# The second modulation's weights loaded ahead of the gathers and in the second front, with front weights in four slots and the first expert weights requested behind its attention

## The chip, the cores and the metric

The kernel runs on one core of a Trainium2 chip. The metric is the time of one execution on the device in microseconds (us). A measurement of it is the median of some runs of the same program. Weights, tables and inputs start in HBM, the output ends there. The core has five engines with a queue of instructions each: PE (matmuls), DVE and ACT (elementwise work, reductions, casts), POOL (it issues the indirect gathers here) and SP (it issues the plain loads). Sixteen DMA engines move all the data. An engine takes its queue in order, so an instruction that waits holds up all that stand behind it.

## The reference, cut to what matters

256 tokens of width 1024 go through two blocks.

```python
# first block (after attention and a recurrent branch)
mod = silu(c) @ w_ada + b_ada                        # 6 x 1024
h2 = rms_norm(x) * (1 + scale2) + shift2
q = (h2 @ w_query).reshape(128, 8, 2, 128)           # 8 heads, two halves
s_top, i_top = top_k(q . sub_keys, 16)               # of 128 keys each
best, pos = top_k(sums of the two, 16)               # of 256 pairs
idx, g = i_top[0] * 128 + i_top[1], softmax(best)    # 16 of 16384 experts
x += gate2 * sum_k g * gelu(x . expert_u[idx]) * expert_v[idx]

# second block
mod_2 = silu(c_2) @ w_ada_2 + b_ada_2                # sh1, sc1, ga1, sh2, sc2, ga2
h = rms_norm(x) * (1 + sc1) + sh1
q, k, v, xb, bg, cg, gates = split(h @ w_in_2)       # 5120 columns
y_a, y_b = attention(rope(q), rope(k), v), gated_conv(xb, bg, cg)
x += ga1 * ((gate_a * (y_a @ w_pa) + gate_b * (y_b @ w_pb)) @ w_o)
x += ga2 * moe(rms_norm(x) * (1 + sc2) + sh2)        # 32 experts, w1, w3, w2
```

The vector c_2 is an input: mod_2 depends on nothing that the first block computes.

## The kernel before

The kernel runs in stages: the first front (`_front1`), the scores of the first expert layer (`_peer_scores`), its experts (`_peer_experts`), the second front (`_front2`) and the second expert layer (`_moe`). All large weights go through one SBUF buffer, `arena`, of eight slots of 128 x 4096 float32 (2 MB, called a piece here); two more slots, 8 and 9, exist only from the second expert layer on. The first is the buffer `room` of the second front under another use.

**Loads.** SP issues every piece in the order of its queue; a load waits until all who used the slot are done, and all loads behind it in the queue wait with it. For the second block `load2` takes slots from a fixed sequence (`ring`, L169): first 3, 4, 5, 6, 0, 7 in turn, then ten slots in turn. It issues a piece when it is first asked for. A scheduler sets the order of the instructions on each engine from the dependences and its own estimates; the order written in the program is where it starts from.

**Gathers.** `_peer_experts` treats each block of 128 tokens in 32 groups of four gathers. A gather (L838) fetches 128 rows of 8 KB, 1.05 MB, each row the two vectors u and v of an expert. Ten buffers take turns: seven quarter-slot pairs in the arena (in slots 0, 1, 5, 6 and 7) and three tiles named `uv`. For each gather PE spreads a token's row over a wide PSUM tile `bc` (L855; there are two of these), DVE multiplies it with u and sums (L857), and for each group PE adds the weighted v into `acc` (L864). The buffer is then free.

**Routing.** The list of picks per block (`route`) is DVE work handed out in small slices by `k.fill`. Block 0's is done in full before the first gather: `k.fill(1e9, (0,))`. It ends with a transpose on PE of the picks (L789), whose copy is the gathers' index table `idx`; a second one (L796) makes the weights `gT`. Block 1's is done beside block 0's groups, a slice of 4.5 us by its own estimate behind each (`k.fill(4.5, (1,))`). Its tables fill slot 4 and part of slot 5. PE's transposes at L811 (`by_tokens`) turn the tokens for the broadcasts.

**Second modulation.** w_ada_2 has twelve pieces. Three calls of `modulation2`, behind groups 4, 12 and 20 of block 0 in program order, take four pieces each through slots 3 and 2 in turn. A piece is eight matmuls (16 rows of the trace, which shows each of these float32 products as two) with c_2's column vectors (`csr2`, L206) into a PSUM bank; behind the fourth, ACT copies the bank (`ada_m`), PE transposes it (L217) and DVE adds the bias into `mod2`. On SP, pieces 0 and 1 are issued at the end of the scores, and the scheduler has put all twelve into the first fifteen groups.

**Second front.** The statistics of x come first (L233, eight matmuls), then the modulated x, then q, k and v (L286 to L288, three matmuls for each product, 144 in all), the rotation of q and k on DVE (L295 to L312), heads (L363), attention, then 14 projections of 48 matmuls each (L273 to L275; the scheduler puts them among the attention), the products with w_pa and w_pb, the router and w_o. The ten pieces of w_in_2 are used in order of their number. The order on PE is the scheduler's.

## Time and profile before

| | |
|---|---|
| time, median of 3 runs | 1730.04 us (1729.21 to 1736.62) |
| the profiled execution, its own time | 1729.57 us |
| its span | 1727.8 us |
| busy: PE, DVE, ACT, POOL | 1319.6, 854.9, 309.2, 241.4 us |
| moved by DMA | 594.56 MB, mean 344 GB/s |
| of these plain loads (queue q1), gathers (q0) | 324.80 MB, 268.45 MB |

The span runs from the first to the last instruction that the profiler saw; the 1.8 us beside it are the start and the end of the execution. A stretch in which the DMA share is 1.00 is one in which all sixteen engines always had a packet to move. The granted clock is that of TensorE, as a share of its full 2.4 GHz.

### The profile page before, as it was taken

The numbers are of one execution on the slowest core, as the hardware profiler recorded it, in microseconds if no ns is written. First come the engines' busy times: TensorE is split into PE (matmuls) and PEld (weight loads), VectorE is DVE, ScalarE is ACT, GpSimd is POOL, SyncE is SP. The second block draws the span as 40 slices with busy tenths as digits, with TensorE's granted clock in tenths as the row PEclk, the third lists the DMA queues.
The fourth block names the chain that finished last, engine by engine and source line by source line (L and its number), as shares of the span: only waits on it lengthen the run. The fifth ranks groups of instructions, "written<-read, shape, count | busy, mean of one in ns | idle before, by whom it ended". The sixth has DMA issues, their size and how long they took to land.

```text
span 1727.8 us, 19564 instructions
## 1 busy us (share of the span) xinstructions
PE 1319.6 (76%) x7782; PEld 775.2 (45%) x7782; DVE 854.9 (49%) x1844; ACT 309.2 (18%) x545; POOL 241.4 (14%) x260
## 2 busy tenths in 40 slices
PE   4999999466777777778767775999989666665765
PEld 2878899322332333333333332799964212221211
DVE  4778778938872454454545454775443211120111
ACT  3566544110000000010000001545230000000000
POOL 0000000033332234333433330000000000000000
PEclk8999999778888889898998887999989978888888
DMA  9467741189999999999999998445479999999997
GB/s 379 191 244 274 307 175 50 49 363 419 420 423 424 420 420 421 420 420 420 420 420 419 420 416 329 154 147 201 145 301 427 428 426 428 427 428 427 427 427 306
DMA packets 64992, 594.56 MB, mean 344 GB/s; under 512 B 7008, under 2 KB 8064, under 8 KB 12672
## 3 DMA queue, kind: packets, MB, share of 16 engines
q1 hardware_dynamic: 28032, 324.80, 46.0%
q0 software_dynamic: 36864, 268.45, 37.5%
q8 instruction: 63, 1.03, 0.2%
q14 instruction: 33, 0.27, 0.0%
HBM read 592.15 MB, written 1.08 MB: 343 GB/s over the span
## 4 chain that ended last, share of the span: by engine, by line
DMA 48%; PE 31%; DVE 13%; issue 3%; ACT 2%; POOL 1%; SPq 0%; DVEq 0%; POOLq 0%; ACTq 0%
DMA arena<-w 18%; DMA arena<-uv,idx 16%; DMA uv<-uv,idx 8%; DMA ring<-w 5%; PE acc L864 4%; PE ps L275 3%; PE ps L273 3%; PE bc L855 3%; PE ps L274 3%; DVE arena L857 3%; DVE wl L262 2%; PE ps L980 2%; DVE uv L857 2%; PE ps L1195 1%; POOL arena L838 1%
## 5 line engine op out<-in xcount | busy, mean ns | idle before, releaser
L855 PE MATMUL bc<-ht,identr 128*128 128x512 f32 x1024 | 336.6, 456 | 173.0 <-DVE arena L857 115.6
L855 PEld LDWEIGHTS bc<-ht,identr 128*128 128x128 f32 x1024 | 189.4, 206 | 358.5 <-DVE arena L857 173.5
L857 DVE SCALAR_TENSOR_TENSOR arena<-arena,bc 128x1024 f32<-128x1024 f32 x181 | 219.7, 1219 | 216.1 <-DMA arena<-uv,idx 136.5
L838 POOL DMA_INDIRECT arena<-uv,idx x181 | 170.3, 941 | 706.1 <-DVE arena L793 348.3
L273 PE MATMUL ps<-hr,wh 128*128 128x256 f32 x648 | 183.3, 283 | 0.9 <-ACT wh L261 0.8
L275 PE MATMUL ps<-hr,wl 128*128 128x256 f32 x648 | 182.0, 281 | 0.4 <-DVE wl L262 0.4
L274 PE MATMUL ps<-hr,wh 128*128 128x256 f32 x648 | 181.9, 281 | 0.0
L262 DVE TENSOR_TENSOR wl<-arena,wh 128x1024 fp32r<-128x1024 f32 (+1 forms) x116 | 139.5, 1213 | 74.4 <-ACT wh L261 73.9
L864 PE MATMUL acc<-arena,wz 128*32 128x512 f32 x724 | 162.4, 776 | 6.0 <-DVE wz L860 6.0
L1195 PE MATMUL ps<-arena,xg 128*32 128x512 f32 x832 | 116.0, 687 | 55.3 <-DMA arena<-w 55.1
L261 ACT CAST wh<-arena 128x1024 fp32r<-128x1024 f32 (+1 forms) x116 | 119.6, 1043 | 137.4 <-PE ps L274 95.4
L857 DVE SCALAR_TENSOR_TENSOR uv<-uv,bc 128x1024 f32<-128x1024 f32 x75 | 91.3, 1219 | 88.6 <-PE bc L855 45.0
L273 PEld LDWEIGHTS ps<-hr,wh 128*128 128x128 f32 x648 | 121.9, 188 | 5.1 <-ACT wh L261 2.3
L275 PEld LDWEIGHTS ps<-hr,wl 128*128 128x128 f32 x648 | 121.8, 188 | 1.6 <-DVE wl L262 0.8
L274 PEld LDWEIGHTS ps<-hr,wh 128*128 128x128 f32 x648 | 121.9, 188 | 0.7 <-issue 0.5
L858 ACT ACTIVATE s<-s 128x4 f32<-128x4 f32 x64 | 13.1, 205 | 606.4 <-DVE arena L857 346.9
L1205 DVE TENSOR_TENSOR hid<-hid,ps 128x512 f32<-128x512 f32 x8 | 5.5, 688 | 211.6 <-PE ps L1195 211.6
L1218 PE MATMUL ps<-arena,hidT 128*32 128x512 f32 x400 | 64.1, 746 | 40.2 <-DMA arena<-w 36.3
L864 PE MATMUL acc<-uv,wz 128*32 128x512 f32 x300 | 94.2, 732 | 0.6 <-DVE wz L860 0.6
L838 POOL DMA_INDIRECT uv<-uv,idx x75 | 71.0, 946 | 94.8 <-PE acc L864 66.6
L1195 PEld LDWEIGHTS ps<-arena,xg 128*32 128x32 f32 x832 | 24.8, 117 | 129.6 <-DMA arena<-w 65.1
L864 PEld LDWEIGHTS acc<-arena,wz 128*32 128x32 f32 x724 | 30.7, 132 | 77.3 <-issue 46.9
(357 smaller groups left out, 1555.4 us busy)
## 6 DMA issues: line engine op xcount, KB each, us to landing
arena<-w SPq DMA_DIRECT2D x73, 2048.0 KB, 39.1
arena<-w_ada SPq DMA_DIRECT2D x24, 2048.0 KB, 11.8
ring<-w SPq DMA_DIRECT2D x19, 2048.0 KB, 39.1
arena<-w_in SPq DMA_DIRECT2D x18, 2048.0 KB, 8.4
arena<-w_query SPq DMA_DIRECT2D x4, 2048.0 KB, 11.2
arena<-w SPq DMA_DIRECT2D x8, 1024.0 KB, 16.2
arena<-w_o_lru SPq DMA_DIRECT2D x2, 2048.0 KB, 10.5
arena<-w_out SPq DMA_DIRECT2D x2, 2048.0 KB, 9.6
```

The costliest lines, as they stand in the source:

```text
L261: nc.scalar.copy(hi, w)
L262: nc.vector.tensor_tensor(lo, w, hi.bitcast(F32), ALU.subtract)
L273: nc.tensor.matmul(out, wh[:, c, cs], rh[:, c, :], start=c == 0, stop=False)
L274: nc.tensor.matmul(out, wh[:, c, cs], rl[:, c, :], start=False, stop=False)
L275: nc.tensor.matmul(out, wl[:, c, cs], rh[:, c, :], start=False, stop=c == kc - 1)
L838: nc.gpsimd.indirect_dma_start(out=uv, out_offset=None, in_=ap["uv"], in_offset=bass.IndirectOffsetOnAxis(ap=idx[:, t:t + 1], axis=0))
L855: nc.tensor.matmul(b[:, 512 * h:512 * h + 512], pick, ht[:, tb, a, 512 * h:512 * h + 512], start=a == 0, stop=a == 1)
L857: nc.vector.scalar_tensor_tensor(u, u, 1.0, b, ALU.mult, ALU.mult, accum_out=s4[:, j:j + 1])
L864: nc.tensor.matmul(acc[32 * j:32 * j + 32, 512 * h:512 * h + 512], w[:, j, 31 - r:63 - r], vs[j][:, 512 * h:512 * h + 512], start=r == 0, ...
L980: nc.tensor.matmul(b[:, j * T:(j + 1) * T], w[:, c, (2 * q + j) * P:(2 * q + j + 1) * P], src[:, c, :], start=c == 0, stop=c == 3)
L1195: nc.tensor.matmul(b[32 * j:32 * j + 32, :], xg[:, c, 32 * j:32 * j + 32], w[:, cc, j, :], start=c == 0, stop=c == NC - 1)
L1218: nc.tensor.matmul(y[h][32 * j:32 * j + 32, :], hidT[:, f, 32 * j:32 * j + 32], w[:, j], start=f == 0, stop=f == 3)
```

## The change

- `csr2` is made from a pool that outlives the stage (`k.persist2`) and is used in both places below.
- In `_peer_experts` the first eight pieces of w_ada_2 go through slots 0, 3, 1, 2 in turn. The first four are asked for between the first `by_tokens` and the filling in of block 0's routing, the next four behind the second `by_tokens`. Their sums lie in the two `bc` tiles until `_ada_set` has read them, the first before the gathers, the second in group 0. `modulation2` and its three calls are gone.
- In `_front2` pieces 8 and 9 come between q, k, v and the rotation in program order, pieces 10 and 11 and the last `_ada_set` behind the attention. Their bank is one of the `ps` banks.
- `load2`'s sequence of slots is new: w_in_2's pieces take 3, 4, 5, 6, 3, 4, 5, 6, 3, 4, the last modulation pieces 0, 7, 0, 7, and the first three pieces of w1 take 0, 7, 8. Pieces 3, 4 and 5 of w_in_2 are asked for before the rotation, piece 6 and the three of w1 right behind the attention. Slot 8 is made there too, in place of `room`.

```diff
--- before.py
+++ after.py
@@ -166,7 +166,8 @@
     def slot(n):
         return k.arena[:, n * 4 * D:(n + 1) * 4 * D] if n < 8 else k.more[n - 8]
 
-    ring = itertools.chain((3, 4, 5, 6, 0, 7) * 2, (3, 4), itertools.cycle((8, 5, 6, 2, 0, 7, 3, 4, 1, 9)))
+    ring = itertools.chain((3, 4, 5, 0, 7, 6, 3, 4, 0, 7, 5, 0, 7, 8, 6, 3, 4, 5, 6, 3, 4),
+                           itertools.cycle((5, 6, 2, 3, 4, 1, 9, 0, 7, 8)))
     ahead = {}
 
     def load2(name, g=None):
@@ -207,10 +208,10 @@
                                  start=c == 0, stop=c == NC - 1)
 
 
-def _ada_set(nc, k, two, b, n, mod=None, bias="b_ada"):
+def _ada_set(nc, k, two, b, n, mod=None, bias="b_ada", tag="proj"):
 
     mod = k.mod if mod is None else mod
-    m = two.tile([P, 512], F32, name="ada_m", tag="proj")
+    m = two.tile([P, 512], F32, name="ada_m", tag=tag)
     nc.scalar.copy(m, b)
     bt = k.pa.tile([P, 512], F32, name="pa", tag="pa")
     for q in range(4):
@@ -812,22 +813,23 @@
                     nc.scalar.copy(ht[:, tb, a, 512 * g:512 * g + 512], b)
 
 
-        csr = _silu_cols(nc, k, one, "c_2", "csr2")
-        ring = itertools.cycle((3, 2))
+        k.csr2 = _silu_cols(nc, k, k.persist2, "c_2", "csr2")
+        ring = itertools.cycle((0, 3, 1, 2))
+        ahead = {}
 
         def load(name, g):
-            w = k.slot(next(ring))
-            nc.sync.dma_start(w, ap[name][g])
-            return w
-
-        def modulation2(n):
-            b = k.pa.tile([P, 512], F32, name="pa", tag="pa")
-            _ada_load(nc, load, csr, b, n, range(4), "w_ada_2")
-            _ada_set(nc, k, one, b, n, k.mod2, "b_ada_2")
+            if g not in ahead:
+                ahead[g] = k.slot(next(ring))
+                nc.sync.dma_start(ahead[g], ap[name][g])
+            return ahead[g]
 
         by_tokens(0)
+        sums = [pb.tile([P, D], F32, name="bc", tag="bc")[:, :512] for _ in range(2)]
+        _ada_load(nc, load, k.csr2, sums[0], 0, range(4), "w_ada_2")
         k.fill(1e9, (0,))
         by_tokens(1)
+        _ada_set(nc, k, one, sums[0], 0, k.mod2, "b_ada_2")
+        _ada_load(nc, load, k.csr2, sums[1], 1, range(4), "w_ada_2")
 
         nv = itertools.cycle((0, 2, 4, 6, 30, 22, 24, None, None, None))
 
@@ -865,8 +867,8 @@
                                          vs[j][:, 512 * h:512 * h + 512], start=r == 0, stop=r == 31)
                 if tb == 0:
                     k.fill(4.5, (1,))
-                    if r in (4, 12, 20):
-                        modulation2(r // 8)
+                    if r == 0:
+                        _ada_set(nc, k, one, sums[1], 1, k.mod2, "b_ada_2")
             if tb == 0:
                 k.fill(1e9, (1,))
             y = _unit(k, 8)
@@ -918,6 +920,10 @@
             for tb in range(2):
                 dst = vv[tb] if n == 2 else qk[tb][:, n]
                 nc.scalar.copy(dst.rearrange("p h e -> p (h e)"), b[tb])
+
+        adab = bank()
+        _ada_load(nc, load, k.csr2, adab, 2, (0, 1), "w_ada_2")
+        wx, wb, wc = (wpiece("w_in_2", 3 + g) for g in range(3))
         work = flat(ybT)
         for tb in range(2):
             cos = k.const("cos2")[:, 8 * tb:8 * tb + 8]
@@ -926,6 +932,14 @@
             _heads_T(nc, k, qk[tb], qT, kT, 64, tb)
         pT = room[:, 3 * D:3584].rearrange("p (h n t) -> p h n t", h=2, n=2)
         _attention(nc, k, one, pT, att_s, qT, kT, vv, 64, 0.125, causal, yaT)
+        _ada_load(nc, load, k.csr2, adab, 2, (2, 3), "w_ada_2")
+        _ada_set(nc, k, two, adab, 2, k.mod2, "b_ada_2", "cg")
+
+
+        wpiece("w_in_2", 6)
+        k.more = [k.extra.tile([P, 4 * D], F32, name="ring0", tag="ring")]
+        for g in range(3):
+            load("w1", g)
 
         def proj(w, q, rh_, rl_):
             b = bank()
@@ -942,7 +956,6 @@
         nc.vector.memset(k.ones16, 1.0)
 
 
-        wx, wb, wc = (wpiece("w_in_2", 3 + g) for g in range(3))
         for q in range(2):
             cg = two.tile([P, 512], F32, name="cg")
             bx = proj(wx, q, hh, hl)
@@ -1043,7 +1056,7 @@
         tc.tile_pool(name="moa", bufs=1) as one,
         tc.tile_pool(name="mod", bufs=1, space=bass.MemoryType.DRAM) as dram,
     ):
-        k.more = [(k.extra, one)[n].tile([P, 4 * D], F32, name=f"ring{n}", tag="ring") for n in range(2)]
+        k.more.append(one.tile([P, 4 * D], F32, name="ring1", tag="ring"))
         iota = k.const("iota")
 
         def small(shape, name, dt=F32):
@@ -1312,6 +1325,7 @@
         _setup(tc, nc, ap, k, pool)
         with tc.tile_pool(name="router", bufs=1) as router:
             _router_setup(k, router)
+            k.persist2 = router
             with contextlib.ExitStack() as stage:
                 with banks(), tc.tile_pool(name="wide", bufs=3) as k.wide:
                     _front1(tc, nc, ap, k)
```

Where the instructions stand now is shown at three places. The first is SP's queue from the last load of the scores (w_query) to the first expert weights (`w`); `masks` and `w_r` are small tables. Before:

```order
L715 DMA arena<-w_query 128x4096
L820 DMA arena<-w_ada 128x4096 x6
L177 DMA arena<-w_in 128x4096
L820 DMA arena<-w_ada 128x4096 x6
L177 DMA arena<-w_in 128x4096 x4
L905 DMA room<-masks 128x128
L177 DMA arena<-w_in 128x4096 x5
L177 DMA arena<-w_pa 128x4096
L177 DMA arena<-w_pb 128x4096
L177 DMA arena<-w_o 128x4096
L939 DMA arena<-w_r 128x320
L940 DMA arena<-masks 128x128
```

After:

```order
L716 DMA arena<-w_query 128x4096
L823 DMA arena<-w_ada 128x4096 x8
L178 DMA arena<-w_in 128x4096 x3
L178 DMA arena<-w_ada 128x4096 x2
L907 DMA room<-masks 128x128
L178 DMA arena<-w_in 128x4096
L178 DMA arena<-w_ada 128x4096
L178 DMA arena<-w_in 128x4096
L178 DMA arena<-w_ada 128x4096
L178 DMA arena<-w_in 128x4096 x2
L178 DMA arena<-w 128x4096 x2
L178 DMA arena<-w_in 128x4096 x3
```

Eight modulation pieces stand in a row ahead of three pieces of w_in, of which the last one waits for the gathers (slot 6); the other four stand among the pieces of w_in behind that one.

The second is PE's queue at the first routing, from the last transposes of the scores (L737, now L738). L812, L857, L207, L790 and L797 are what L811, L855, L206, L789 and L796 were. Before:

```order
L737 MATMUL ps<-arena 128x128 x8
L811 MATMUL pa<-consts,hr 128x128 x8
L855 MATMUL bc<-ht,identr 128x512 x8
L789 MATMUL pa<-consts,arena 128x128
L811 MATMUL pa<-consts,hr 128x128 x7
L796 MATMUL pa<-consts,arena 128x128
L811 MATMUL pa<-consts,hr 128x128 x9
L206 MATMUL pa<-arena,csr_2987 32x512 x9
```

After:

```order
L738 MATMUL ps<-arena 128x128 x8
L812 MATMUL pa<-consts,hr 128x128 x8
L207 MATMUL bc<-arena,csr_2987 32x512 x40
L857 MATMUL bc<-ht,identr 128x512 x4
L207 MATMUL bc<-arena,csr_2987 32x512 x8
L790 MATMUL pa<-consts,arena 128x128
L812 MATMUL pa<-consts,hr 128x128 x4
L207 MATMUL bc<-arena,csr_2987 32x512
L812 MATMUL pa<-consts,hr 128x128 x4
L207 MATMUL bc<-arena,csr_2987 32x512 x7
L812 MATMUL pa<-consts,hr 128x128 x3
L797 MATMUL pa<-consts,arena 128x128
```

The transpose of the picks (L789, L790) stood behind transposes and broadcasts alone; now 48 of the modulation's matmuls, six pieces, stand ahead of it, and the broadcasts of the first gather behind the fifth piece.

The third is PE's queue at the start of the second front, from the last group's sum (L864, now L866): the transposes of its result, the statistics (L233, now L234) and the first product for q. Before:

```order
L864 MATMUL acc<-arena,wz_2980 32x512 x8
L878 MATMUL pa<-consts,arena 128x128 x8
L233 MATMUL pa<-arena,consts 128x256 x8
L286 MATMUL pa<-wh,hr 128x512
L287 MATMUL pa<-wl,hr 128x512
L288 MATMUL pa<-wh,hr 128x512
```

After:

```order
L866 MATMUL acc<-arena,wz_2980 32x512 x8
L880 MATMUL pa<-consts,arena 128x128 x8
L207 MATMUL ps<-arena,csr_2987 32x512 x8
L234 MATMUL pa<-arena,consts 128x256 x8
L207 MATMUL ps<-arena,csr_2987 32x512 x8
L287 MATMUL pa<-wh,hr 128x512
L288 MATMUL pa<-wl,hr 128x512
L287 MATMUL pa<-wh,hr 128x512
```

Piece 8's matmuls stand ahead of the statistics and piece 9's behind them. Pieces 10 and 11 stand behind the first heads (L364, sixteen transposes, one matmul among them), and the heads of the second token block stand behind 34 projection matmuls where they stood behind 98.

## Rows read from the trace of the kernel before

**Rows 1.** The page's slices: the whole span in 40 equal parts of 43.2 us, the busy share of the 16 DMA engines in tenths and what they moved in each.

```profile
DMA  9467741189999999999999998445479999999997
GB/s 379 191 244 274 307 175 50 49 363 419 420 423 424 420 420 421 420 420 420 420 420 419 420 416 329 154 147 201 145 301 427 428 426 428 427 428 427 427 427 306
```

**Rows 2.** The page's chain of work that ended last, followed back from the end: shares of the span, first by engine, then by line.

```profile
DMA 48%; PE 31%; DVE 13%; issue 3%; ACT 2%; POOL 1%; SPq 0%; DVEq 0%; POOLq 0%; ACTq 0%
DMA arena<-w 18%; DMA arena<-uv,idx 16%; DMA uv<-uv,idx 8%; DMA ring<-w 5%; PE acc L864 4%; PE ps L275 3%; PE ps L273 3%; PE bc L855 3%; PE ps L274 3%; DVE arena L857 3%; DVE wl L262 2%; PE ps L980 2%; DVE uv L857 2%; PE ps L1195 1%; POOL arena L838 1%
```

**Rows 3.** The table of stretches, from ahead of the gathers to the experts' stage. Columns: stretch and length in us, then busy us and number of instructions of PE, PE's weight loads, DVE, ACT and POOL, the granted TensorE clock, the DMA share and GB/s.

```profile
318.00:347.00 29.00, 2.06 (x9) 1.15 (x8) 27.64 (x79) 2.09 (x3) 0.00 (x0) 0.58 0.03 12
348.00:400.00 52.00, 35.23 (x151) 13.89 (x149) 21.00 (x68) 4.93 (x9) 15.16 (x16) 0.79 0.96 392
400.00:500.00 100.00, 71.30 (x292) 34.97 (x292) 88.33 (x255) 1.85 (x9) 36.70 (x38) 0.85 1.01 421
500.00:580.00 80.00, 61.23 (x293) 22.26 (x294) 27.74 (x55) 5.08 (x10) 15.83 (x17) 0.87 1.01 423
580.00:1040.00 460.00, 347.87 (x1477) 154.96 (x1475) 234.31 (x422) 13.32 (x50) 171.66 (x184) 0.88 1.01 420
1040.00:1075.00 35.00, 18.61 (x73) 8.62 (x70) 16.09 (x32) 7.22 (x11) 1.87 (x2) 0.73 0.77 307
1075.00:1290.00 215.00, 202.74 (x1429) 183.81 (x1431) 128.99 (x250) 85.83 (x145) 0.00 (x0) 0.96 0.51 190
1290.00:1717.00 427.00, 286.72 (x1894) 101.01 (x1886) 75.18 (x192) 21.30 (x45) 0.00 (x0) 0.88 1.00 424
```

**Rows 4.** The timeline of SP, which issues the weights' loads: start of the first and time to the last issue of the group, line, what, number of loads.

```profile
283.69 28.77 SPq L820 DMA_DIRECT2D arena<-w_ada  x2
354.72 28.70 SPq L820 DMA_DIRECT2D arena<-w_ada  x4
...
480.42 0.33 SPq L177 DMA_DIRECT2D arena<-w_in  x1
508.56 42.40 SPq L820 DMA_DIRECT2D arena<-w_ada  x6
562.12 0.33 SPq L177 DMA_DIRECT2D arena<-w_in  x1
```

**Rows 5.** The table of stretches by group of four gathers, block 0's groups 13 to 16; a stretch goes from the end of one group's last L864 matmul to the end of the next one's.

```profile
516.00:534.80 18.80, 11.77 (x74) 4.32 (x66) 3.94 (x8) 0.79 (x2) 3.75 (x4) 0.91 1.00 422
534.80:552.50 17.70, 13.91 (x68) 4.31 (x64) 5.08 (x9) 0.20 (x1) 3.75 (x4) 0.90 1.01 424
552.50:578.20 25.70, 17.76 (x72) 5.57 (x68) 6.47 (x13) 0.79 (x2) 3.75 (x4) 0.80 1.01 423
578.20:588.30 10.10, 8.27 (x45) 4.04 (x38) 5.08 (x9) 0.20 (x1) 4.53 (x5) 0.99 1.01 419
```

**Rows 6.** The page's DMA issues: KB of each and the median us from issue to landing.

```profile
arena<-w SPq DMA_DIRECT2D x73, 2048.0 KB, 39.1
arena<-w_ada SPq DMA_DIRECT2D x24, 2048.0 KB, 11.8
```

**Rows 7.** The timeline of PE around the first routing: start, length, line, what, number; in brackets the idle time before it and what ended it.

```profile
317.88 2.17 PE L855 MATMUL bc<-ht,identr 128*128 128x512 f32 x8
347.05 0.45 PE L789 MATMUL pa<-consts,arena 128*128 128x128 f32 x1 [26.99 <-DVE arena L788]
...
352.42 3.08 PE L206 MATMUL pa<-arena,csr 128*32 128x512 f32 x18
```

**Rows 8.** The timeline of POOL, which issues the gathers.

```profile
348.73 1.08 POOL L838 DMA_INDIRECT arena<-uv,idx  x1 [348.27 <-DVE arena L793]
...
351.35 0.94 POOL L838 DMA_INDIRECT arena<-uv,idx  x1 [0.30 <-issue]
...
377.73 0.94 POOL L838 DMA_INDIRECT arena<-uv,idx  x1 [16.73 <-DVE arena L699]
```

**Rows 9.** DVE's costliest groups of instructions by line between 400 and 500 us: busy us, mean ns of one, idle us before it and what ended that.

```profile
L857 DVE SCALAR_TENSOR_TENSOR arena<-arena,bc 128x1024 f32<-128x1024 f32 x28 | 33.6, 1209 | 4.7 <-DMA arena<-uv,idx 3.6 <-PE bc L855 1.0
L857 DVE SCALAR_TENSOR_TENSOR uv<-uv,bc 128x1024 f32<-128x1024 f32 x11 | 13.2, 1211 | 2.4 <-PE bc L855 2.4
```

**Rows 10.** The timeline of PE at the start of the second front, and at the heads of its second token block.

```profile
1070.02 1.97 PE L878 MATMUL pa<-consts,arena 128*128 128x128 f32 x8 [1.16 <-ACT arena L873]
1073.81 5.12 PE L233 MATMUL pa<-arena,consts 128*128 128x256 f32 x16 [1.82 <-DVE arena L232]
1082.35 0.50 PE L286 MATMUL pa<-wh,hr 128*128 128x512 f32 x1 [3.41 <-ACT hr L247]
...
1131.52 2.00 PE L363 MATMUL pa<-consts,room 128*64 128x128 f32 x16 [0.32 <-DVE room L312]
```

**Rows 11.** The table of stretches inside the second front, columns as above.

```profile
1082.00:1087.00 5.00, 4.65 (x13) 3.45 (x14) 4.90 (x13) 2.87 (x8) 0.00 (x0) 0.66 0.01 2
1087.00:1272.00 185.00, 183.93 (x1322) 169.88 (x1321) 110.83 (x168) 75.69 (x123) 0.00 (x0) 1.00 0.49 184
```

**Rows 12.** The chain of work, its part in the first front: start, length, what, number.

```profile
177.46 2.71 PE ps L206 x24
```

**Rows 13.** The timeline of SP where the gathers end.

```profile
1040.23 29.05 SPq L177 DMA_DIRECT2D arena<-w_in  x3
```

**Rows 14.** The chain of work at the first experts' matmuls.

```profile
1286.53 13.91 PE ps L1195 x128
```

## The prediction

> **What bounds the kernel now.** I read the page's slices first: the DMA line stands at 9 from slice 10 to slice 24 and again from slice 31 to the last but one, and the GB/s line shows some 420 there against 50 in slices 7 and 8 [rows 1]. The chain that ended last agrees: 48% of the span is DMA, above all the gathers and the expert weights [rows 2]. The table of stretches then gives each stage its own limit [rows 3]. From 348 to 1040 us, the gather stage, the DMA share is 0.96 to 1.01 at 392 to 423 GB/s; it is just as full with modulation weights in it (500 to 580) as without (580 to 1040). From 1290 on the experts' weights fill the DMA again at 424. Between these lies the second front (1075 to 1290): PE is busy 202.74 of 215 us, and the DMA has a share of 0.51. Ahead of the gathers, 318 to 347 us, PE has 2.06 us of work, DVE 27.64, and the DMA moves 12 GB/s: DVE's routing of block 0 sets the time. So two stretches are bound by bytes, one by PE, one by DVE, and a byte taken out of the first kind and put into either of the others should be worth its time on the full engines.
>
> **What leaves the gather stretch.** SP's issues show where the twelve pieces of the second modulation go now: two are issued from 283.69 to 312, four from 354.72 to 383, six from 508.56 to 551, with a piece of w_in at 480.42 and another at 562.12 [rows 4]. Only the first two modulation pieces are out before the gathers start at 348.73 [rows 8]; ten go through the full stretch, and so does the w_in piece of 562.12, which had to wait for slot 3, the modulation's. After the change eight pieces go through four slots before the gathers. The loads into slots 0, 1, 2 can start as the front and the scores leave them, and the second four as PE finishes with the first four. The w_in piece for slot 3 then follows right behind, also before the gathers. The w_in piece of 480.42 waits for block 1's routing tables in slot 4 as before and stays. So eleven pieces leave: ten of w_ada_2 and one of w_in.
>
> A piece is 128 x 4096 x 4 B = 2.097 MB. At the mean of 421 and 423 GB/s [rows 3] it takes 4.97 us of the sixteen engines, eleven take **54.7 us**. A second way checks it: the three groups that carry the later modulation took 18.80, 17.70 and 25.70 us where the next takes 10.10 [rows 5], an excess of 31.9 us for the later seven pieces, some of whose bytes fall in the group ahead; 7 x 4.97 is 34.8. Bounds from the slowest and the fastest of these rows (419 and 424): 54.4 to 55.1.
>
> The Trainium skill ("DMA: Bandwidth & Descriptors", section Where 436 GB/s comes from) holds that loads from HBM are bound at about 358 GB/s per core. By that a piece would take 5.86 us and eleven would bring 64.4 us, an estimate from that page; the rows read 420 to 424 GB/s, above it, so the rows decide and the sum goes by them.
>
> **Beside the first routing.** The eight pieces need 8 x 4.97 = 39.8 us of DMA, and with the w_in piece 44.7. Four can go before 318 us: today's second issue is at 312 already [rows 4], and the four slots are last read by the front and the scores. From 318 on, five are left, 24.9 us, which fit into the 29 us at 12 GB/s [rows 3]. On PE a piece is 16 rows of the trace: the nine matmuls that the order shows as one run were 18 rows in 3.08 us [rows 7], 0.171 each, so 2.7 us a piece and 21.9 for eight, in the 26.99 us that PE sits idle before 347.05 [rows 7]. The new order puts six pieces, 16.4 us, ahead of the transpose that turns block 0's picks into gather indices. Counting from 319 us, where PE is free today, pieces 0 and 1 are done at 321.7 and 324.4; pieces 4 and 5 are asked for then and land, at the 11.8 us that such pieces take [rows 6], at 333.5 and 336.2, or one load behind, 338; PE is done with them by 341. The transpose is due at 347.05, so 6 us are spare. This I cost at **0**; its cover is DVE's routing, and without that margin every microsecond that load six is late delays the first gather by one. Pieces 6 and 7 stand among the transposes behind it and hold slots 1 and 2; slot 1 takes the third gather, issued at 351.35 [rows 8], and piece 6's 2.7 us of matmuls lie between 347 and then: 0 to 3 us on the start, of which I take 0, because ten gathers stand in the queue at once. The sigmoid product of c_2 goes to the program's start: four small operations, 0.
>
> **The first groups, where DVE is nearly full.** With the bytes out, groups 0 and 1 should run at 10 us a group. Between 400 and 500 DVE is 88.33 us busy in 100 [rows 3] while the DMA stays at 1.01, and DVE's score products waited 3.6 us for gathers and 1.0 for PE only [rows 9]. Each group carries the same slice of block 1's routing, so DVE needs about 9.3 us of a 10.5 us group: the DMA remains last, by a microsecond. Two of the sums now hold both wide PSUM buffers until about 350 us, so PE cannot make the broadcasts of group 0 early as it does at 317.88 [rows 7]; they are due when the first gather lands (its 1.05 MB alone are 2.5 us) and take 1.1 us per buffer [rows 7]. 0, at most 2 us.
>
> **The second front.** Four pieces (8.4 MB) move here, into a stretch with DMA to spare. On PE come four pieces' matmuls and 4 transposes. Pieces 8 and 9 stand before and behind the statistics, where PE is idle 1.82 and 3.41 us [rows 10], and take 1.8 us each by the first front's 24 rows in 2.71 us [rows 12] or 2.7 by the slower rows above: 0 to 0.9, I take **0.5**, if the pieces have landed. Their slots 0 and 7 were the last but one and the last that the gathers left for w_in, issued between 1040.23 and 1069.3 [rows 13], and at 1082 nothing was left in flight (DMA share 0.01 [rows 11]). So piece 9 can be late by up to 2 us. Pieces 10 and 11 stand where PE has no gap (183.93 of 185 us [rows 11]): 32 rows at 0.113 are **3.6 us**; four transposes **0.5**, half of what they would take by the 1.97 for 8 at the lower clock [rows 10]. The heads of block 1 stand 64 projections earlier than before on PE; today PE waits 0.32 us there for DVE's rotation at 1131.52 [rows 10], and then it would wait longer: 0 to 6 us, I take **1.5**, since the new order gives DVE the rotation earlier too, but not by as much. The clock between 1082 and 1087 was granted at 0.66 and behind that at 1.00 [rows 11]; extra matmuls in the gaps may bring the rise forward, -2.4 to 0 us, I take 0. The w_in pieces go through four slots; each is requested when the piece four before it is done on PE, and with two projection groups (11 us) between request and use against a load time of some 5 us at a share of 0.51 they are in time: 0, at most 5. Sum **+6.1**, from -2.4 to about +16.
>
> **The experts.** The first three weight pieces are requested earlier, but the stage starts with its ten slots full today: its first 128 matmuls run without a break in 13.91 us [rows 14]. What starts at 1290 is a stream at 424 GB/s that ends when the bytes end; more could be loaded ahead only with more slots. **0**.
>
> **Sum.** The profiled run took 1729.57 us, of which 1727.8 are the span; 1729.57 - 54.7 + 6.1 = **1681.0**. The median of the runs shown is 0.5 higher; I leave it at **1681 us**.
>
> **Rivals.**
> *A. The first four pieces' time is not given back.* Buffers come free in bursts: after ten gathers POOL waits 16.73 us until 377.73 [rows 8]. If DVE, with its 9.3 us of work a group, becomes the last in groups 0 and 1, 20 of the 54.7 us are lost: 1701. For it: the 88.33. Against: gathers queued ahead are 10 x 2.5 = 25 us of DMA, and groups 2 to 10 run at 1.01 DMA with that same DVE load. Chance 0.07.
> A rule of the Trainium skill points the same way ("SBUF — State Buffer", section Who interferes with whom): GpSimd is locked out of writing descriptors while DVE runs certain copies, casts and scalar operations. POOL's issues took 0.97 us in the stretch with DVE at 88%, and 0.93 where DVE is at half [rows 3]; the trace does not bear it out beyond 0.04 us each.
> *B. The second front stalls.* A late modulation piece holds PE's whole queue, since the attention and all projections stand behind it: +10 to 15 us more than I count, 1694. For it: pieces 10 and 11 are issued only when two w_in pieces have gone. Against: the share of 0.51. Chance 0.07, inside the range.
> *C. The stretch is not bound by bytes* but by each gather's own handling, so that freed time is left idle. Then only the front's cost remains: 1736. Against: the groups with pieces are longer by just the pieces' time [rows 5]. Chance 0.03.
> *D, the other side: the six loads hold up the routing.* PE executes in order, and the picks' transpose stands behind load six. If a piece needed 39.1 us, as expert weights do under a full queue, instead of w_ada's 11.8 [rows 6], and four followed each other from 317, the sixth would land at 473 and all gathers start 126 us later: 1807. It decides from load six landing 49 us after the picks, near 396; then the result is slower than before. Against: 12 GB/s in that stretch. Chance 0.03.
>
> **How the numbers follow.** My case has 0.80. Its bounds are 1672 (55.1 out, front -2.4) and 1696 (54.4 out, front +16, start 5). B lies inside, A at 1701, C and D far off. The range 1670 to 1697 takes in my case and B; A, C and D, 0.13, lie outside, and some more of my case may. A measurement of this kernel can tell about 0.5% (9 us) from no change: faster 0.94 (mine, A, B), same 0.03 (C), slower 0.03 (D).
>
> **What would show it.** Eight w_ada issues before 330 us, and the DMA busy from 318 to 347; the first gather still at 348 to 351. Groups 0, 1 and 12 to 15 at about 10 us each, 419 to 424 GB/s throughout, and the transposes behind the last group near 1015 instead of 1070.02 [rows 10]. PE from there to the first expert matmul 6 us longer than now, and the experts' stage unchanged. It would be wrong if the first gather came later than 355, if the DMA share in groups 0 to 10 fell under 0.95, or if PE had gaps of over 5 us at the heads or projections.

## The result, and the profile after

| | median | runs | ratio to the kernel before, 95% interval |
|---|---|---|---|
| before | 1732.95 us | 1729.21 to 1736.62 | |
| the change | 1683.08 us | 1681.67 to 1686.42 | 0.9719 [0.9699, 0.9739] |
| forecast | 1681 us | 1670 to 1697 | |

The kernel before has four runs here; the median of 1730.04 us given ahead is that of three of them. The profiled run of the change took 1682.16 us with a span of 1680.3. The table of stretches of the changed kernel, columns as in [rows 3]:

```profile
318.00:347.00 29.00, 14.74 (x111) 4.55 (x109) 27.73 (x81) 2.49 (x5) 0.00 (x0) 0.81 0.91 374
348.00:360.00 12.00, 11.73 (x63) 5.15 (x61) 3.56 (x10) 5.81 (x8) 6.69 (x7) 0.80 0.77 267
360.00:400.00 40.00, 29.89 (x128) 13.36 (x126) 33.50 (x114) 0.82 (x4) 14.35 (x16) 0.87 1.01 421
400.00:500.00 100.00, 73.98 (x302) 38.23 (x302) 86.69 (x229) 4.72 (x12) 37.70 (x39) 0.83 1.01 421
500.00:580.00 80.00, 54.23 (x256) 25.02 (x255) 40.61 (x72) 1.64 (x8) 31.46 (x34) 0.96 1.01 420
580.00:990.00 410.00, 306.60 (x1316) 139.01 (x1315) 207.94 (x374) 12.30 (x45) 150.79 (x161) 0.88 1.01 419
...
1020.00:1235.00 215.00, 205.12 (x1448) 183.79 (x1447) 131.83 (x260) 87.97 (x146) 0.00 (x0) 0.98 0.61 234
1240.00:1665.00 425.00, 288.05 (x1898) 101.92 (x1894) 75.22 (x192) 21.31 (x45) 0.00 (x0) 0.87 1.01 423
```

From 318 to 347 the DMA moves 374 GB/s where it moved 12, and PE has 14.74 us of work there. From 360 to 990 the DMA share is 1.01 at 419 to 421 GB/s, with or without the first groups' routing on DVE (86.69 us busy in 100). The second front (1020 to 1235) now moves 234 GB/s for 190, and the experts' stage is as it was. The timeline of SP shows where the pieces went, to set beside [rows 4, 13]:

```profile
273.16 53.37 SPq L823 DMA_DIRECT2D arena<-w_ada  x8
335.87 0.33 SPq L178 DMA_DIRECT2D arena<-w_in  x1
...
462.88 526.12 SPq L178 DMA_DIRECT2D arena<-w_in  x2
998.25 20.43 SPq L178 DMA_DIRECT2D arena<-w_ada  x2
```

Eight modulation pieces are issued by 326.5 and a piece of w_in at 335.87; of the twelve pieces that stood in the gather stage one is left, that of 462.88 (the second of its group of two is the piece at the end of the gathers; it waits for slot 5, not for slot 6 as said ahead). POOL's gathers, to set beside [rows 8]:

```profile
348.94 1.07 POOL L840 DMA_INDIRECT arena<-uv,idx  x1 [348.48 <-PE pa L812]
350.31 0.93 POOL L840 DMA_INDIRECT arena<-uv,idx  x1 [0.30 <-issue]
353.92 0.94 POOL L840 DMA_INDIRECT arena<-uv,idx  x1 [2.67 <-PE bc L207]
...
370.97 0.94 POOL L840 DMA_INDIRECT arena<-uv,idx  x1 [7.43 <-DVE arena L700]
```

The first starts as before (348.94 against 348.73), the third 2.6 us later, and the eleventh, which waits for a buffer to come free, at 370.97 where it was 377.73. PE ahead of it, to set beside [rows 7]:

```profile
319.06 7.07 PE L207 MATMUL bc<-arena,csr 128*32 128x512 f32 x64
329.00 3.55 PE L207 MATMUL bc<-arena,csr 128*32 128x512 f32 x16 [2.86 <-DMA arena<-w_ada]
...
333.88 1.93 PE L207 MATMUL bc<-arena,csr 128*32 128x512 f32 x16 [0.20 <-DMA arena<-w_ada]
347.23 0.47 PE L790 MATMUL pa<-consts,arena 128*128 128x128 f32 x1 [11.43 <-DVE arena L789]
...
351.38 2.60 PE L207 MATMUL bc<-arena,csr 128*32 128x512 f32 x14
```

Piece 5 is done at 335.81 and PE waits 11.43 us for the picks: the cover held, with more to spare than the 6 us that I worked out. Piece 6's matmuls end at 353.98, and the third gather starts with that. PE at the start of the second front, to set beside [rows 10]:

```profile
1019.41 1.09 PE L880 MATMUL pa<-consts,arena 128*128 128x128 f32 x8 [1.16 <-ACT arena L875]
1020.44 1.92 PE L207 MATMUL ps<-arena,csr 128*32 128x512 f32 x16
1022.75 3.69 PE L234 MATMUL pa<-arena,consts 128*128 128x256 f32 x16 [0.39 <-DVE arena L233]
1026.37 1.92 PE L207 MATMUL ps<-arena,csr 128*32 128x512 f32 x16
1029.86 0.50 PE L287 MATMUL pa<-wh,hr 128*128 128x512 f32 x1 [1.56 <-ACT hr L248]
...
1065.59 3.63 PE L207 MATMUL ps<-arena,csr 128*32 128x512 f32 x30
...
1073.32 1.47 PE L364 MATMUL pa<-consts,room 128*64 128x128 f32 x12
```

The transposes start at 1019.41 (before: 1070.02). Pieces 8 and 9 take 1.92 us each, the statistics 3.69 us for the same 16 rows that took 5.12, and the first product starts 10.45 us behind the transposes where it was 12.33. The heads of the second token block (1073.32) have no wait. The granted clock in the table of stretches, first the kernel before, then the change:

```profile
1070.00:1082.00 12.00, 7.09 (x24) 5.58 (x24) 5.83 (x18) 3.63 (x7) 0.00 (x0) 0.72 0.86 348
```

```profile
1019.00:1030.00 11.00, 8.64 (x57) 4.80 (x58) 6.54 (x21) 4.50 (x9) 0.00 (x0) 1.00 0.98 389
1030.00:1035.00 5.00, 5.00 (x23) 4.08 (x24) 5.00 (x13) 3.82 (x8) 0.00 (x0) 1.00 0.96 408
```

It is 1.00 from the transposes through the first products, where it was 0.72 up to the first product and 0.66 in the next 5 us [rows 11], a mean over time at 1.2 and at 2.4 GHz.

### The profile page after: what moved, and what is told of

It reads as the page before. It is cut to its first block, busy times and chain, and to the rows that moved or that the text cites. A ratio compares the mean times of both kernels' runs of the same rounds, so it can differ in the third digit from the quotient of the medians.

```text
span 1680.3 us, 19564 instructions
## 1 busy us (share of the span) xinstructions
PE 1301.6 (77%) x7782; PEld 777.2 (46%) x7782; DVE 855.5 (51%) x1844; ACT 308.9 (18%) x545; POOL 242.1 (14%) x260
## 4 chain that ended last, share of the span: by engine, by line
DMA 43%; PE 37%; DVE 13%; issue 3%; ACT 2%; POOL 1%; SPq 0%; DVEq 0%; POOLq 0%; ACTq 0%
DMA arena<-w 19%; DMA arena<-uv,idx 12%; DMA uv<-uv,idx 9%; PE bc L857 4%; PE ps L274 4%; PE ps L276 4%; PE ps L275 4%; PE acc L866 4%; DVE arena L859 4%; DMA ring<-w 2%; PE ps L1208 2%; DVE uv L859 2%; PE ps L993 2%; PE pa L1141 1%; DVE wl L263 1%
## 5 line engine op out<-in xcount | busy, mean ns | idle before, releaser
L857 PE MATMUL bc<-ht,identr 128*128 128x512 f32 x1024 | 334.8, 455 | 172.9 <-DVE arena L859 114.6
L857 PEld LDWEIGHTS bc<-ht,identr 128*128 128x128 f32 x1024 | 191.1, 207 | 346.5 <-DVE arena L859 168.0
L859 DVE SCALAR_TENSOR_TENSOR arena<-arena,bc 128x1024 f32<-128x1024 f32 x181 | 219.9, 1219 | 170.0 <-PE bc L857 88.4
L274 PE MATMUL ps<-hr,wh 128*128 128x256 f32 x648 | 185.7, 287 | 0.0
L275 PE MATMUL ps<-hr,wh 128*128 128x256 f32 x648 | 184.5, 285 | 0.0
L866 PE MATMUL acc<-arena,wz 128*32 128x512 f32 x724 | 153.5, 736 | 6.5 <-DVE wz L862 6.5
L274 PEld LDWEIGHTS ps<-hr,wh 128*128 128x128 f32 x648 | 124.1, 192 | 5.1 <-issue 2.8
L275 PEld LDWEIGHTS ps<-hr,wh 128*128 128x128 f32 x648 | 124.1, 192 | 0.9 <-issue 0.8
L866 PE MATMUL acc<-uv,wz 128*32 128x512 f32 x300 | 90.8, 711 | 0.6 <-DVE wz L862 0.5
L866 PEld LDWEIGHTS acc<-arena,wz 128*32 128x32 f32 x724 | 29.1, 127 | 74.7 <-issue 44.8
```

The costliest lines, as they stand in the source:

```text
L274: nc.tensor.matmul(out, wh[:, c, cs], rh[:, c, :], start=c == 0, stop=False)
L275: nc.tensor.matmul(out, wh[:, c, cs], rl[:, c, :], start=False, stop=False)
L857: nc.tensor.matmul(b[:, 512 * h:512 * h + 512], pick, ht[:, tb, a, 512 * h:512 * h + 512], start=a == 0, stop=a == 1)
L859: nc.vector.scalar_tensor_tensor(u, u, 1.0, b, ALU.mult, ALU.mult, accum_out=s4[:, j:j + 1])
L866: nc.tensor.matmul(acc[32 * j:32 * j + 32, 512 * h:512 * h + 512], w[:, j, 31 - r:63 - r], vs[j][:, 512 * h:512 * h + 512], start=r == 0, ...
```

## The experiments

Each kernel has one profiled execution, from which these stretches are read: first gather on POOL to the transposes, from there to the first experts' matmul in the chain, and from there to the end. All in us.

| kernel | ratio [95%] | first gather | gathers | front | experts |
|---|---|---|---|---|---|
| before | | 348.73 | 721.3 | 216.5 | 441.3 |
| before again | 1.0001 [0.9984, 1.0019] | 348.32 | 721.5 | 216.2 | 441.3 |
| the change | 0.9719 [0.9699, 0.9739] | 348.94 | 670.5 | 218.8 | 442.1 |
| the change again | 0.9722 [0.9694, 0.9750] | 349.98 | 668.0 | 219.7 | 443.9 |
| first part | 0.9840 [0.9815, 0.9865] | 349.46 | 687.0 | 219.8 | 444.0 |
| second part | 0.9916 [0.9897, 0.9936] | 349.06 | 703.7 | 219.9 | 444.2 |
| slots only | 1.0034 [1.0015, 1.0052] | 350.31 | 723.9 | 218.9 | 444.1 |
| no gap matmuls | 0.9766 [0.9748, 0.9785] | 351.12 | 665.7 | 228.1 | 444.0 |
| gather order | 0.9722 [0.9703, 0.9741] | 349.17 | 662.1 | 221.1 | 442.6 |
| four more loads | 0.9918 [0.9900, 0.9937] | 349.33 | 700.4 | 219.9 | 442.2 |
| y in slot 4 | 0.9690 [0.9673, 0.9707] | 351.53 | 666.5 | 219.7 | 442.2 |
| both | 0.9693 [0.9671, 0.9715] | 349.61 | 665.0 | 221.8 | 443.1 |
| unused matmuls | 1.0059 [1.0022, 1.0097] | 350.85 | 720.2 | 225.9 | 443.8 |
| unused, spread | 0.9987 [0.9977, 0.9997] | 348.23 | 719.6 | 213.0 | 441.4 |

The theory: each piece that leaves the gather stage is worth its time on the full DMA engines, wherever it goes, and the second front pays only for matmuls on PE. The rivals: the first groups give nothing back (DVE), the gain comes from slots and early requests, or late pieces stall the front.

**Two kernels again,** with no edit.

> The kernel before, unchanged, to see how much the length of each stretch differs between two executions: first gather to the last transposes 721 us, first product to the experts 204 us, experts to the end 441 us, each within 1 us if the stretches repeat. If the experts' stage takes 444 us here, the 2 to 3 us by which the kernels with one part of the change were longer there are the execution's and not theirs.

> The changed kernel, unchanged, for the same purpose: first gather to the last transposes 670 us, first product to the experts 208.4 us, experts to the end 442 us. Bytes theory: the stretch of the gathers is 50 to 55 us shorter than in the kernel before on the same chip, whatever the rest does.

The kernel before repeats to 0.4 us in every stretch; the change to 2.5 us in the gathers and 1.9 in the experts' stage, which has 441.3 to 444.2 us in all kernels of the table, also in one with the loads of the kernel before (unused matmuls, 443.8). The kernel before did not show 444 us itself, but the change gives 442.1 and 443.9 with the same instructions. Differences of 2 to 3 us in the gathers or the experts' stage of one execution are therefore not explained below; the front differs by 0.3 and 0.9 us between the two executions of one kernel. The gathers are 50.8 us shorter in the first pair and 53.4 in the second.

**The first part alone.**

```diff
-        ring = itertools.cycle((0, 3, 1, 2))
+        ring = itertools.chain((0, 3, 1, 2) * 2, itertools.cycle((3, 2)))
...
+                    if r == 20:
+                        modulation2(2)
```

The lines for pieces 8 to 11 in `_front2` and their slots are left out, and `modulation2` is that of the kernel before.

> Eight modulation pieces ahead of the gathers as in the change; pieces 8 to 11 through slots 3 and 2 into the gather stage, and nothing of the modulation in the second front. Bytes theory: of the twelve pieces that the kernel before sends through the gather stage (ten of the modulation, two of w_in) five or six stay, so six to seven leave, at 4.97 us each 30 to 35 us; the second front costs nothing more than before: ratio 0.980 to 0.983. Rival A (time freed in the first groups is not given back): only what leaves the later groups counts, about 10 us, ratio 0.994. Rival (the gain comes from the second front's slots and early requests, which this kernel has too): the whole gain, 0.972.

Five pieces are issued into the gather stage, so seven of twelve left it. The gathers are 34.3 us shorter, 4.9 a piece: as the bytes theory has it, and rival A (10 us) falls. The whole gain of 0.972, which the rival of the slots and early requests expects, does not come either. But the time is 1.6% less where 1.7 to 2.0 was expected (the interval reaches to 1.85), and front and experts took 6 us more.

**The second part alone.**

```diff
-        ring = itertools.cycle((0, 3, 1, 2))
+        ring = itertools.cycle((3, 2))
...
+                    if r in (4, 12):
+                        modulation2(r // 8)
```

> Pieces 0 to 7 as in the kernel before (through slots 3 and 2, two of them ahead of the gathers), pieces 8 to 11 in the second front as in the change. Bytes theory: four of twelve pieces leave the gather stage, 19.9 us, and the front costs the 2.3 us that it costs in the change: 17.6 us, ratio 0.990. Rival (DMA spare capacity in the second front is an illusion, late pieces stall PE there): ratio 0.995 or above, with PE gaps of over 5 us between the first product and the experts.

Four pieces left, 17.6 us of gathers, 4.4 a piece. The interval of the ratio holds the bytes theory's 0.990 and not the rival's 0.995, and there are no PE gaps of 5 us in the front. Front and experts took 6.3 us more than before, 3.4 of them in the front, where the change takes 2.3 and 3.5 more.

**The slots and early requests alone** (the edit is shown against the kernel before).

```diff
-    ring = itertools.chain((3, 4, 5, 6, 0, 7) * 2, (3, 4), itertools.cycle((8, 5, 6, 2, 0, 7, 3, 4, 1, 9)))
+    ring = itertools.chain((3, 4, 5, 6, 3, 4, 5, 0, 7, 8, 6, 3, 4, 5, 6, 3, 4),
+                           itertools.cycle((5, 6, 2, 3, 4, 1, 9, 0, 7, 8)))
```

The early requests for w1 and for w_in's pieces come with it, and so does the new place of `csr2`; `modulation2` stays in its three places.

> The modulation as in the kernel before, all twelve pieces in the old places; only the second front's slots (four for w_in) and the early requests of three expert pieces are those of the change. Bytes theory: the same bytes in the gather stage, the experts' stage starts with ten full slots either way: ratio 1.000, within 0.002. Rival (early expert requests bring time at the experts' stage): up to three pieces, 15 us, ratio 0.991. Rival (two expert pieces now stand ahead of w_in in the queue and hold up the second front): 1.002 to 1.006.

0.34% slower, 5.9 us, with an interval clear of 1: the last rival's size, and against my 0. The profiled execution spreads it over all stretches (gathers 2.5, front 2.5, experts 2.8, start 1.6). Those of gathers and experts are as large as two executions of the change differ, but the front's can be placed. From the end of the products for q, k and v to the last projection the four executions with the old slots (before, before again and the two with unused matmuls below) took 152.3 to 152.4 us, this one 154.1. PE waits less in it (0.5 us for 1.1), so the rival's way, a front held up by its loads, is not what the trace shows; the 864 projection matmuls themselves take longer, 104.8 us for 102.3. Twenty us of projections in the table of stretches, of the kernel before, of this one and of the change:

```profile
1190.00:1210.00 20.00, 20.00 (x174) 20.00 (x173) 8.58 (x7) 9.25 (x11) 0.00 (x0) 1.00 0.54 215
```

```profile
1196.00:1216.00 20.00, 20.00 (x169) 20.00 (x168) 8.58 (x7) 8.67 (x11) 0.00 (x0) 1.00 0.51 202
```

```profile
1140.00:1160.00 20.00, 20.00 (x169) 20.00 (x168) 8.58 (x7) 8.83 (x10) 0.00 (x0) 1.00 0.47 181
```

At the same granted clock 169 matmuls start where 174 did: one follows the other after 0.120 us (median) in all ten executions with the new slots and after 0.117 in the four with the old. Why is open; the slots of the weights and the place of `csr2` both changed. Most of the rest of the front's 2.5 us lies ahead of the first product, which comes 13.09 us behind the transposes (12.33 and 11.94 before).

With this as the base the parts add up: first part 33.6 us (1.94% of 1731), second part 20.4 (1.18%), by the bytes 34.8 and 19.9, and 5.9 - 33.6 - 20.4 = -48.1 us against the change's -48.6. Each of these differences has an interval of some 5 us to either side, so the closeness is partly luck.

**No matmuls in the gaps.**

```diff
-    ring = itertools.chain((3, 4, 5, 0, 7, 6, 3, 4, 0, 7, 5, 0, 7, 8, 6, 3, 4, 5, 6, 3, 4),
-                           itertools.cycle((5, 6, 2, 3, 4, 1, 9, 0, 7, 8)))
+    ring = itertools.chain((3, 4, 5, 0, 7, 6, 3, 4, 5, 3, 4, 5, 3, 0, 7, 6, 4, 5),
+                           itertools.cycle((8, 3, 0, 7, 6, 2, 4, 5, 1, 9)))
...
-        _ada_load(nc, load, k.csr2, adab, 2, (0, 1), "w_ada_2")
...
-        _ada_load(nc, load, k.csr2, adab, 2, (2, 3), "w_ada_2")
+        _ada_load(nc, load, k.csr2, adab, 2, range(4), "w_ada_2")
```

The early requests for w1 are left out too.

> The changed kernel with pieces 8 and 9 in slots 3 and 4, so that their matmuls stand behind the products for q, k and v instead of beside the statistics; the slots of the other pieces of the second front are shifted to suit, and the early expert requests are gone. Clock theory (matmuls in the gaps bring the granted clock up before the first product, which is what kept the front at +2.3 instead of +6.1 us): the statistics' 16 rows take 5.1 us again instead of 3.7, the clock from the first product on is below 0.7 for some 5 us, and pieces 8 and 9 cost 3.6 us where PE has no gap: 5 to 7 us slower than the change, ratio to before 0.975 to 0.976. Rival (the front's smaller cost has nothing to do with the clock): 1 to 2 us, 0.973.

PE's timeline of this kernel:

```profile
1016.82 1.09 PE L880 MATMUL pa<-consts,arena 128*128 128x128 f32 x8 [1.17 <-ACT arena L875]
1020.16 6.36 PE L234 MATMUL pa<-arena,consts 128*128 128x256 f32 x16 [2.24 <-DVE arena L233]
1029.93 0.79 PE L287 MATMUL pa<-wh,hr 128*128 128x512 f32 x1 [3.41 <-ACT hr L248]
...
1068.37 5.35 PE L207 MATMUL ps<-arena,csr 128*32 128x512 f32 x46
```

The statistics take 6.36 us (3.69 in the change, 5.12 in the kernel before), the first product starts 13.11 us behind the transposes, and the front is 9.2 us longer than in the change: 2.7 ahead of the first product, 2.7 in the products for q, k and v, of which the first thirteen take 0.63 us or more, and most of the rest for pieces 8 and 9 where PE has no gap (3.6). The time is 8 us above the change. More than expected, and other slots changed with it, so this run bears the clock theory out without isolating it.

**Unused matmuls in the gaps of the kernel before.**

```diff
+                if tb + g == 2:
+                    idle = k.pa.tile([P, 512], F32, name="pa", tag="pa")
+                    for _ in range(8):
+                        nc.tensor.matmul(idle[:32, :], k.ident[:, :32], y[:, :512], start=True, stop=True)
```

Eight more of half the width stand behind the statistics.

> The kernel before with sixteen matmuls that nobody uses: eight behind the last transposes, eight of half the width behind the statistics, in the two gaps of PE where the change puts pieces 8 and 9; no load is moved. Clock theory: the statistics' 16 rows take 3.7 to 4.0 us instead of 5.1, the first products run at 0.39 us from the start instead of 0.63 for five us, and the first product to the experts takes 2 to 2.5 us less, with more work on PE: total 0 to 3 us below the kernel before, ratio 0.998 to 1.000. Rival (PE pays for the extra matmuls): 2 to 4 us above, ratio 1.001 to 1.002.

PE's timeline:

```profile
1072.93 8.68 PE L885 MATMUL pa<-arena,consts 128*32 128x512 f32 x16 [0.79 <-DVE xT L889]
1081.66 3.72 PE L233 MATMUL pa<-arena,consts 128*128 128x256 f32 x16
...
1093.62 0.79 PE L289 MATMUL pa<-wh,hr 128*128 128x512 f32 x1 [4.66 <-ACT hr L250]
```

Both expectations missed. The matmuls took 8.68 us where pieces 8 and 9 take 1.92: all write the same 32 partitions of a bank, at a granted clock of 0.81. The eight of half the width behind the statistics, in one group too, took 3.64 us at 1.00, so the clock is not the main part of it. The statistics came at 3.72 us, but behind the extra matmuls PE was idle for 4.66 us, since the statistics' reader on ACT waited for them (its first instruction behind the statistics starts at 1089.03, when the last of them is done), and the first products were back at 0.79 and 0.63 us. So they were spread over four groups of 32 partitions, as the modulation's are, in a bank of their own:

```diff
-                        nc.tensor.matmul(idle[:32, :], k.ident[:, :32], y[:, :512], start=True, stop=True)
+                        j = n % 4
+                        nc.tensor.matmul(idle[32 * j:32 * j + 32, :], k.ident[:, :32], y[:, :512], start=n < 4, stop=n >= 4)
```

> As the run with sixteen unused matmuls, but spread over the four column groups of PE as the modulation's are (16 rows in 1.9 to 2.7 us, where those in one group took 8.68), and in a bank of their own, so that the statistics' reader does not wait for them. Clock theory: statistics in 3.7 us instead of 5.1, first products at 0.39 us from the start; from the transposes to the first product 10.5 to 11.5 us (12.33 and 11.94 in the two executions of the kernel before), and from there to the experts 202 to 203 (204.2): 1 to 3 us less in all, with more work on PE; the total within 0.2% of the kernel before. Rival (PE pays for the extra matmuls): 2 to 4 us more in these two stretches.

```profile
1069.73 1.92 PE L889 MATMUL pa<-arena,consts 128*32 128x512 f32 x16 [0.79 <-DVE xT L893]
1071.74 3.72 PE L233 MATMUL pa<-arena,consts 128*128 128x256 f32 x16
1075.39 1.92 PE L238 MATMUL pa<-arena,consts 128*32 128x512 f32 x16
1078.88 0.50 PE L292 MATMUL pa<-wh,hr 128*128 128x512 f32 x1 [1.56 <-ACT hr L253]
```

Transposes to first product 11.03 us, from there to the experts 202.0 (before: 204.2 twice). The kernel before became 0.13% faster by work that nobody uses, with an interval that ends at 0.9997. The rival falls. The other kernels agree: the statistics take 3.7 to 4.0 us in all eight executions that have matmuls spread over four groups in both gaps, and 5.1 to 6.7 in the five that have none. The products for q, k and v take 33.9 us in this run for 35.6 in the kernel before, and with the new slots 33.0 with matmuls in the gaps for 35.7 to 35.9 without. What stands in those gaps is worth some 3 us of front, whatever it computes, if it does not itself leave PE idle ahead of the first product as the sixteen in one group did.

**The gathers' buffers in another order.**

```diff
-        nv = itertools.cycle((0, 2, 4, 6, 30, 22, 24, None, None, None))
+        nv = itertools.cycle((0, 2, 30, 22, 24, None, None, None, 4, 6))
```

> The changed kernel with the gathers' buffers in another order: those in slot 1, which the modulation's piece 6 holds until 353.92, come ninth and tenth in place of third and fourth. Theory (the part of the gain that is missing, 4.1 of 54.7 us up to the transposes, is in part the third gather's wait): gathers 3 to 8 are issued 1.24 us apart right behind the second, the third at 351.6; DMA share from 348 to 360 up from 0.77 to 0.85 or more, 2 to 2.6 us faster than the change, ratio to before 0.970 to 0.971. Rival (the wait is hidden, since the queue never runs dry): no difference, 0.972.

POOL's timeline:

```profile
350.55 0.94 POOL L840 DMA_INDIRECT arena<-uv,idx  x1 [0.31 <-issue]
351.79 0.94 POOL L840 DMA_INDIRECT arena<-uv,idx  x1 [0.30 <-issue]
...
360.49 0.93 POOL L840 DMA_INDIRECT arena<-uv,idx  x1 [0.31 <-issue]
```

The third gather no longer waits, and all ten are out 2.1 us earlier, but the DMA share from 348 to 360 is 0.76, as in the change. Its profiled execution was the shortest of its five; the ratio is that of the change. No gain that can be told: inconclusive at this size, with the rival's figure.

**Four more loads ahead of the gathers.**

```diff
         _ada_load(nc, load, k.csr2, sums[0], 0, range(4), "w_ada_2")
+        ahead.clear()
+        _ada_load(nc, load, k.csr2, sums[0], 0, range(4), "w_ada_2")
```

> The changed kernel with pieces 0 to 3 loaded and multiplied twice, so twelve pieces (8.4 MB more) stand ahead of the gathers, the output being the same. Theory (that stretch is now full at 374 GB/s, and the four slots turn no faster than PE and DMA let them): 4 x 4.9 us less the little that is left free, 10 to 19 us slower than the change, ratio 0.978 to 0.983, the first gathers issued late or the late pieces among them. Rival (there was more room beside the routing, and eleven pieces are a limit only of the slots): under 4 us, 0.974 or less.

33 us slower than the change, twice what was expected. PE and then POOL:

```profile
347.66 0.45 PE L790 MATMUL pa<-consts,arena 128*128 128x128 f32 x1 [11.28 <-DVE arena L789]
...
362.88 1.92 PE L207 MATMUL bc<-arena,csr 128*32 128x512 f32 x16
385.81 2.07 PE L859 MATMUL bc<-ht,identr 128*128 128x512 f32 x4 [21.01 <-DVE arena L861]
```

```profile
363.74 0.94 POOL L842 DMA_INDIRECT uv<-uv,idx  x1 [0.30 <-issue]
390.05 0.94 POOL L842 DMA_INDIRECT arena<-uv,idx  x1 [25.37 <-PE bc L207]
```

The picks are on time (347.66), but PE's queue has broadcasts between the late pieces. The broadcast at 385.81 waits 21.01 us for DVE, which waits 24.3 us for a gather that shares the DMA engines with the late loads (share 1.01 from 357 to 377); the pieces behind it on PE hold slots, and the gathers for these slots wait 25.37 us. By the stage's rate 20 of the 33 us are the bytes. The rest fits this ring of waits, in which the DMA share falls to 0.84 (360 to 400 us, 344 GB/s) and 0.75 (400 to 430, 295 GB/s): at 421 GB/s that is some 16 us lost, against some 5 gained from 347 to 360, where it moves 411 GB/s for the change's 251.

**The last piece.**

```diff
-            y = _unit(k, 8)
+            y = _unit(k, 16)
```

> The changed kernel with the tile y (the group sum on its way to the transposes) in slot 4 in place of slot 2, so that the w_in piece for slot 4, which the change still issues at 462.88 into the gather stage, cannot start before the second block's transposes. Bytes theory: one piece more leaves the gather stage, 4.6 to 4.9 us; the second front has room, and the piece is needed some 11 us behind the first product: 4 to 5 us faster than the change, ratio to before 0.969 to 0.970. Rival (the twelfth piece comes late in the second front, behind three others issued at once): the products for k wait 3 to 8 us, no gain or a loss, 0.972 to 0.974.

SP's timeline:

```profile
338.54 649.38 SPq L178 DMA_DIRECT2D arena<-w_in  x2
997.83 19.42 SPq L178 DMA_DIRECT2D arena<-w_ada  x2
...
1020.04 0.81 SPq L178 DMA_DIRECT2D arena<-w_in  x2
```

The piece that the change issues at 462.88 now goes at 1020.04, and no piece is left in the gather stage ahead of its last groups. Its ratio is 0.9690 against 0.9719 and 0.9722, 5 us, with intervals that overlap; the gathers of its execution are 4.0 us shorter than the change's first and 1.5 than its second. The theory's figure, with the next kernel the lowest of all; but with overlapping intervals a gain over the change is likely and not shown.

> Both edits of the two kernels before: the gathers' buffers in another order, and y in slot 4. If they are independent, 6 to 7.5 us faster than the change: ratio 0.968 to 0.969. If only one of them works, its own figure.

0.9693: the slot edit's figure alone.

## Why the prediction was right

1. *Eleven pieces, 54.7 us.* The term that decides was right in kind and within 7% in size: 50.8 and 53.4 us in the two pairs of executions, 34.3 for seven pieces, 17.6 for four. That is 4.4 to 4.9 us a piece against the 4.97 forecast. The rates of the stage are the same without the pieces (419 to 421 GB/s), so the rows' rate was right. By the 358 GB/s of the Trainium skill ("DMA: Bandwidth & Descriptors", section Where 436 GB/s comes from) seven pieces would have been worth 41 us, an estimate from that page; the trace does not agree with it.
2. *Beside the routing, 0.* The first gather did not move and 11.43 us of PE's wait are left. The third gather's 2.6 us lie in the 0 to 3 that I gave, and taking them away brought no gain that can be told. Rival D's mechanism never came into play at eight pieces, and the run with twelve shows the wait that does come, at another place: broadcasts and pieces that wait for each other through slots.
3. *The first groups.* Rival A fell: the DMA is full from 360 on with DVE at 87% from 400 to 500. POOL's issues take 0.99 us there (mean of 39) and 0.94 from 580 to 990 (mean of 161), so DVE's work held up the gathers' issues by 0.05 us each at most.
4. *The second front, +6.1.* It measured +2.3 and +3.5, and its terms were sized less well than the sum. Pieces 10 and 11 took 0.121 us a row where I had 0.113 (30 rows in 3.63; all 32 in 4.5 for my 3.6). The heads' wait of 1.5 was 0. The term that I mis-sized most is the clock, which I took at 0 between -2.4 and 0. It was worth some 3 us, beyond its bound: granted 1.00 from 1019 to 1035 where it had been 0.72 and 0.66, and in the run with the spread unused matmuls the front is 3.2 and 3.5 us shorter than in the two executions of the kernel before. The low end of the sum was added up wrongly as well: the lowest values of its terms give 3.6 + 0.5 - 2.4 = +1.7, not -2.4, and the range of my case would have begun at 1676, not 1672. Against the clock stands what I put at 0:
5. *Slots and early requests, 0, at most 5.* Alone they cost 5.9 us [1.0015, 1.0052], more than my bound, though the interval reaches below it. Late loads, which I had in mind there, are not what the trace shows: the projections' matmuls follow each other 0.003 us later, 2.5 us in all, of which 0.6 come back as shorter waits. Where the rest of the 5.9 us lies is open. The total came out right (48.6 us below the kernel before by the ratio, 48.6 forecast) in part by luck, because this and the clock lean opposite ways.
6. *The experts, 0.* 442.1 and 443.9 against 441.3 twice: up to 2.6 us more, within what this stage varies among kernels with the same loads. Early requests brought nothing that can be told, as forecast.

Rivals B and C fell with the rows: PE is busy 37.1 of 37.1 us from the first product on and 79.9 of the next 80, and the freed time was used.

## What to carry to other kernels

Where one stage is full on the DMA engines and another is not, a load is priced by the stage it is in: bytes over the measured rate, and look for the slots that let it leave. Before filling the idle engine of a latency-bound stretch, list what stands behind the new work on each queue and which buffers it holds: eight pieces were free, the four beyond them cost 33 us where their bytes are 20. A short gap on PE just ahead of a long run of matmuls is not empty: here the matmuls in it decided the clock at which the run started.

## What the runs showed of the hardware that was not expected

- Sixteen rows of matmuls with 32 output partitions took 8.68 us into one group of partitions (granted clock 0.81) and 1.92 us spread over four (1.00); sixteen of half the width into one group took 3.64 us at 1.00.
- A kernel with sixteen more matmuls, unused, ran in 0.9987 [0.9977, 0.9997] of its time: statistics at 3.72 us for 5.12, first products at 0.50 and 0.40 us, at a granted clock of 1.00 where it had been 0.72 and 0.66. In the run with 4.66 us of idle time ahead of the first product, the products ran at 0.79 and 0.63 us.
- The start of the first gather differs between kernels that are the same up to it by up to 2.6 us (348.94 in the change, 351.53 with y in slot 4), and so do the gathers and the experts' stage; a claim of 2 us there needs many executions, not one profile. The stretch from the products for q, k and v to the last projection repeats to 0.01 us in either kernel (152.27 and 152.28, 158.92 and 158.93).
- The same projection matmuls follow each other after 0.117 us with the old slots and 0.120 with the new, at a granted clock of 1.00; the reason is open.
